# The last layer norm of an expert layer in three steps per unit, with GpSimd's instructions in a set order

## Chip, cores and metric

One core of one Trainium2 chip runs the whole program. The metric is the device time of one execution in microseconds (us). The engines are PE (TensorE), DVE (VectorE), ACT (ScalarE), POOL (GpSimd) and SP (SyncE, which issues plain DMAs). Each executes its own instructions in order, and the engines meet at semaphores.

## What is computed

Two transformer blocks on 2048 tokens of width 1024, all in float32. The first has chunked spatial gating, sliding-window attention and memory cross-attention, the second an mLSTM mixer, a memory cross-attention and a mixture of experts. The change touches only the experts' part and the layer norm behind it:

```
ff = grouped_moe(x, router_w, router_bias, w_gate, w_up, w_down)
x  = layer_norm(DEEPNORM_ALPHA * x + ff, ln_moe_g, ln_moe_b)
```

In `grouped_moe` every token first picks one of four groups of four experts, then two experts of that group. An expert is silu(x W_gate) * (x W_up), then W_down, with inner width 256. The sum is weighted by the two gates, added to ALPHA * x and normalized per token.

## The kernel before

The first part of the program (up to about 2230 us) works through blocks of 512 tokens and leaves three things in DRAM: `x3d` (input rows of the experts with their gates), `sumd` (ALPHA * x, onto which experts add), and tables of token numbers, 128 to a column. `moe()` then runs the experts.

**Units.** An expert has two or three blocks of 128 tokens (`BLOCKS`, 39 in all). Two blocks make a unit; a third block makes a short unit of its own that shares the expert's weights (`of`). There are 23 units, numbered 0 to 22. Units 5, 9, 13, 15, 17, 19 and 21 are short; unit 22 is expert 15, which has two blocks.

**One turn of the loop in `run`** handles unit i. PE does the first half of i's up projection (`up(0)`), then the second (`up(1)`), then the transposes of unit i+1, then the down projection of unit i-1. Around it stand, in program order: the down weights of unit i-1 (`weights_down(1)`) and of unit i; `mids[i]`; the activation; the gather of unit i+2 (`gather`, L1126, by indirect DMA from `x3d`); the scatter-add of unit i-1 onto `sumd` (L1201, one indirect DMA per block); `late[i]`; the up weights of unit i+2. Weights are split into two rounded parts: ACT casts (L173), DVE subtracts (L174). For `weights_down(1)` of experts 4 to 14 POOL subtracts.

**The last norm.** The tokens of experts 0 to 3 form list 0, those of 4 to 7 list 1, 8 to 11 list 2, 12 to 14 list 3, and all that picked expert 15 list 4. A list has `NFIN` static tiles of 128 rows; a list that is longer is finished in a loop behind, together with experts that have more tokens than their blocks hold. When a list's experts are all scattered, `group_done` makes its tiles ready. A tile costs one fetch from `sumd` (L1395, an indirect DMA by POOL), statistics (two L1410 and L1411 on DVE, or two ACT passes L1405 and L1406), the reciprocal root on POOL (`rstd_pow`, L192 and L194), two passes on DVE (L1417 and L1418, the second needs POOL's root) and a scatter to the output (L1419).

`last_norm`, called in `mids` or `late` about once per expert as the table `FETCH` says, finishes an older tile and fetches the next:

```python
            while got and got[0][0] <= t - lag:
                finish([got.pop(0)[1]])
            for _ in range(min(n, len(ready))):
                got.append((t, fetch(ready.pop(0), mem)))
```

**What sets the order.** ACT's and DVE's instructions of the experts' part stand as the program writes them (`manual_schedule` with `MANUAL`). Those of POOL, PE and SP are placed by the scheduler, within the dependencies. On `sumd` these are waits: a fetch waits until the scatter-adds issued before it have landed (`adds`), and a scatter-add waits until earlier scatter-adds and fetches have landed (`adds + reads`).

Of the kernel before, what the change touches and what calls it, by code (L numbers as in the profile page):

```python
# [17 lines left out]
OP = mybir.AluOpType  # L18
AX = mybir.AxisListType

D = 1024
S = 2048
# [5 lines left out]
LN_EPS = 1e-5  # L28
# [8 lines left out]
POOL_FIRST = 1  # L37
MANUAL = "Activation", "DVE"
BLOCKS = 2, 2, 2, 2, 3, 2, 2, 3, 2, 2, 3, 3, 3, 3, 3, 2
FETCH = {5: (1, 0), 6: (1, 0), 7: (1, 0), 8: (1, 0), 9: (1, 1), 10: (1, 0), 11: (1, 0), 12: (1, 0), 13: (1, 1), 14: (1, 1), 15: (1, 0)}  # L40


def f32(ap):
    return ap.bitcast(F32)
# [7 lines left out]
def model(ctx, tc, A, out, taps=None, nsb=NSB, upto=9):  # L52
# [116 lines left out]
    def split(hi, lo, src, lo_eng=None, hi_eng=None):  # L169
        if hi_eng is DVE:  # L170
            DVE.tensor_copy(hi, src)
        else:
            ACT.copy(hi, src)  # L173
        (lo_eng or DVE).tensor_sub(lo, src, f32(hi))  # L174

    def wload(src, w, lo_eng=None, into=None):
        raw = rawload(src, w)
# [9 lines left out]
        mm(o, lh, rl, False, False)  # L187
        mm(o, ll, rh, False, stop)

    def rstd_pow(src, eps, name, scale=1.0, n=1, bufs=3):  # L190
        v = sml([128, n], name + "v")
        POOL.tensor_scalar(v, src, scale, eps, op0=OP.mult, op1=OP.add)  # L192
        r = sml([128, n], name, bufs=bufs)
        POOL.tensor_tensor(r, v, mhalf[:, :n], op=OP.pow)  # L194
        return r

    pending = []
# [740 lines left out]
    NMAX = 28  # L938

    NL = 5  # L940
    NFIN = 4, 5, 5, 4, 2
    if upto >= 3:
        rw = cload("router_w", [128, 8, 16])
        rbias = const.tile([128, 16], F32, name="rbias")
# [139 lines left out]
    def moe():  # L1084
# [19 lines left out]
        def after(a, b):  # L1104
            tc.add_manual_dep(a.ins, b.ins.name, mybir.DependencyInfo(mybir.DependencyClass.Sync,
                                                                      mybir.DependencyReason.DATA), reason="same tokens")

        class Unit:


# [26 lines left out]
            def weights_down(self, f):  # L1137
                if self.of:
                    return
                raw = rawload(self.src_d(f), 1024)  # L1140
                h, l = DW((128, 1024)), DW((128, 1024))
                split(h, l, raw, POOL if self.late and f in LATE_POOL else self.lo)
                self.dw.append((h, l))

            def transposed(self):
# [43 lines left out]
            def down(self):  # L1189
                new = []  # L1190
                for r in range(self.n):
                    rs = slice(r * 128, (r + 1) * 128)
                    y = YT((128, D))
                    for hf in range(2):
                        hs = slice(hf * 512, (hf + 1) * 512)
                        a = acc()
                        for f in range(2):
                            h, l = self.dw[f]
                            mm3(a, self.th[:, f, rs], self.tl[:, f, rs], h[:, hs], l[:, hs], f == 0, f == 1)
                        ACT.activation(y[:, hs], a, AF.Copy, scale=self.gc[r])  # L1200
# [6 lines left out]
                    new.append(d)  # L1207
                adds[:] = new
                reads.clear()

        def run(units, early=None, mids={}, late={}, hooks={}):
            n = len(units)
            for j in range(min(2, n)):
                units[j].gather()
            units[0].weights_up(range(4))
            units[0].transposed()
            if early:
                early()
            if n > 1:
                units[1].weights_up(range(3))  # L1220
            for i, u in enumerate(units):
                v = units[i + 1] if i + 1 < n else None
                w = units[i + 2] if i + 2 < n else None
                u.up(0)
                if i:
                    units[i - 1].weights_down(1)
                u.weights_down(0)
                u.act(0)
                if i:
                    units[i - 1].turn()  # L1230
                if not v:
                    if i:
                        units[i - 1].down()
                    u.weights_down(1)
                if i in mids:
# [157 lines left out]
        def fetch(at, mem):  # L1393
            x = mem((128, D))
            d = POOL.indirect_dma_start(out=x, out_offset=None, in_=sumd[:, :], in_offset=at)  # L1395
            for o in adds:
                after(d, o)
            reads.append(d)
            return x, at

        def stats(x, on):
# [10 lines left out]
            return (mv[:, 0:1], OP.add if on is ACT else OP.subtract,  # L1412
                    rstd_pow(mv[:, 1:2], LN_EPS, "fr", scale=1.0 / D if on is ACT else 1.0))

        def finish(tiles, ons=(DVE,), static=True):
            for (x, at), (mean, op, r) in zip(tiles, [stats(x, on) for (x, at), on in zip(tiles, ons)]):
                DVE.scalar_tensor_tensor(x, x, mean, gains[:, 0], op0=op, op1=OP.mult)  # L1417
                DVE.scalar_tensor_tensor(x, x, r, gains[:, 1], op0=OP.mult, op1=OP.add)  # L1418
                d = POOL.indirect_dma_start(out=out[:, :], out_offset=at, in_=x, in_offset=None,  # L1419
                                            bounds_check=S - 1, oob_is_err=False)  # L1420
                for o in outs:
                    (apart if static else after)(d, o)
                outs.append(d)

        ready, got = [], []
# [5 lines left out]
        def last_norm(t, n, mem=FX, lag=2):  # L1431

            while got and got[0][0] <= t - lag:
                finish([got.pop(0)[1]])
            for _ in range(min(n, len(ready))):
                got.append((t, fetch(ready.pop(0), mem)))

        units, mids, late, hooks = [], {}, {}, {}
        for e in range(16):
            if e in FETCH and e < 15:  # L1440
                for j in range(2):
                    (late if j else mids)[len(units)] = lambda e=e, j=j: last_norm(2 * e + j, FETCH[e][j])
            units.append(static(e, 0, 2))
            if e in (4, 8, 12):
                hooks[len(units) - 1] = [lambda e=e: group_done((e - 1) // 4)]
            if BLOCKS[e] == 3:
                units.append(static(e, 2, 1, units[-1]))
        tables = [group_ranks, *(lambda j=j: place(range(4 * j, 4 * j + 4)) for j in range(4)), placed]
        for j, fn in enumerate(tables):
            mids[j] = fn  # L1450
        hooks.setdefault(5, []).append(overflow_table)
        hooks.setdefault(7, []).append(group_owners)

        def last():
            last_norm(30, 1)
            group_done(3)
            last_norm(0, NFIN[3], XG)

        mids[len(units) - 1] = last
        with tc.manual_schedule(engines={getattr(mybir.EngineType, e) for e in MANUAL}):  # L1460
            run(units, None, mids, late, hooks)
        group_done(4)
        last_norm(0, NFIN[4], MRAW)
        while got:
            finish([f for _, f in got[:2]], (DVE, ACT))
            del got[:2]
        assert not ready and not got


        nit = nc.values_load(ov["nit"][0:1, 0:1], min_val=0, max_val=NMAX)  # L1470
# [108 lines left out]
```

## Time and profile before

| what | value |
|---|---|
| median of three runs | 2713.98 us (2713.91, 2713.98, 2725.86) |
| the profiled execution | 2722.46 us, of which the span is 2720.7 us |
| busy in the span | PE 94%, DVE 59%, ACT 42%, POOL 22% |
| mean granted clock of TensorE | 0.972 of full speed |

The span runs from the first instruction to the last. Busy shares are means over the whole program; the part that the change touches is its last fifth. The profile names for each idle stretch what ended it. A TensorE clock of 1.00 is the level of 2.4 GHz, 0.50 that of 1.2 GHz; values between them are means over a stretch in which it was at both.

### The profile page before, as it was taken

The page shows a single profiled execution, that of the slowest core. Times are in us where ns is not written, and L with a number is a line of the kernel's source. Part 1 is how long each engine was busy: PE and PEld are TensorE (multiplying, and loading weights), DVE is VectorE, ACT ScalarE, POOL GpSimd, SP SyncE. Part 2 cuts the span into 40 slices and gives each one's busy share as a digit, 9 for nine tenths or more (in the row PEclk, how much of TensorE's full clock was granted, in tenths as well). Part 3 has the DMA queues.
Part 4 walks back from the last instruction along what each step waited for, and adds up shares of the span by engine and source line. Part 5 has one row for each costly group of instructions (what it writes and reads, how often), then busy time and mean ns, then how long its engine had stood idle before and what let it go on. Part 6 is the DMA issues. An engine that isn't in the chain of part 4 may idle for free. (4 is left out here: it accounts for less than half of the span.)

```text
span 2720.7 us, 36998 instructions
## 1 busy us (share of the span) xinstructions
PE 2549.0 (94%) x13954; PEld 2156.0 (79%) x13954; DVE 1608.8 (59%) x3228; ACT 1136.1 (42%) x2023; POOL 597.4 (22%) x635
## 2 busy tenths in 40 slices
PE   8899999999999999999999999999999969989882
PEld 8777788777878887778788878778888859978872
DVE  5536366766454666665456666563667457666554
ACT  5644353242444532434354333343532325444442
POOL 0102202211021031101201221021032133445445
PEclk9999999999999999999999999999999979999986
DMA  8861351444224325441242345312415357878755
GB/s 299 287 217 55 109 163 55 154 152 145 92 77 133 117 64 169 155 141 48 84 161 72 116 144 197 94 55 87 162 47 183 104 180 264 247 237 254 223 153 138
DMA packets 121557, 396.81 MB, mean 146 GB/s; under 512 B 15264, under 2 KB 15408, under 8 KB 121376
## 3 DMA queue, kind: packets, MB, share of 16 engines
q1 hardware_dynamic: 104144, 334.01, 36.6%
q0 software_dynamic: 17232, 60.42, 8.4%
q8 instruction: 110, 1.80, 0.3%
q14 instruction: 71, 0.58, 0.1%
HBM read 314.87 MB, written 81.60 MB: 146 GB/s over the span
## 5 line engine op out<-in xcount | busy, mean ns | idle before, releaser
L183 PE MATMUL bank<-rounded 128*128 128x512 f32 (+2 forms) x10628 | 2198.8, 364 | 73.4 <-ACT rounded L173 54.1
L183 PEld LDWEIGHTS bank<-rounded 128*128 128x128 f32 x10628 | 1773.3, 192 | 380.4 <-ACT rounded L173 61.5
L174 DVE TENSOR_TENSOR rounded<-work,rounded 128x1024 fp32r<-128x1024 f32 (+3 forms) x531 | 577.7, 1100 | 476.4 <-ACT rounded L173 430.4
L173 ACT CAST rounded<-work 128x1024 fp32r<-128x1024 f32 (+3 forms) x564 | 512.5, 926 | 691.2 <-PE bank L183 251.8
L173 ACT CAST rounded<-bank 128x512 fp32r<-128x512 f32 (+1 forms) x220 | 112.0, 555 | 219.1 <-PE bank L240 98.1
L183 PE MATMUL bank<-work 128*128 128x128 f32 (+5 forms) x944 | 163.6, 301 | 6.9 <-DVE work L525 2.2
L183 PEld LDWEIGHTS bank<-work 128*128 128x128 f32 (+1 forms) x944 | 130.7, 190 | 37.0 <-issue 5.1
L174 DVE TENSOR_TENSOR rounded<-bank,rounded 128x512 fp32r<-128x512 f32 (+1 forms) x220 | 133.0, 639 | 42.5 <-ACT rounded L173 40.6
L240 PE MATMUL bank<-ident,work 128*128 128x128 f32 x712 | 98.2, 283 | 28.4 <-ACT work L345 8.6
L240 PEld LDWEIGHTS bank<-ident,work 128*128 128x128 f32 x712 | 82.2, 145 | 46.3 <-ACT work L345 13.4
L192 POOL TENSOR_SCALAR lnrv<-lnmv 128x1 f32<-128x1 f32 x32 | 40.6, 1269 | 283.3 <-DVE lnmv L672 283.1
L375 POOL TENSOR_SCALAR work<-work 128x512 f32<-128x512 f32 x32 | 25.4, 793 | 345.9 <-ACT work L374 345.9
L665 DVE SCALAR_TENSOR_TENSOR work<-work,bank 128x512 f32<-128x512 f32 x64 | 43.8, 685 | 73.3 <-PE bank L183 73.1
L1201 POOL DMA_INDIRECT sumd<-work,tabi x39 | 72.1, 1849 | 35.1 <-ACT work L1200 15.7
L174 POOL TENSOR_TENSOR rounded<-work,rounded 128x1024 fp32r<-128x1024 f32 (+1 forms) x33 | 65.9, 1997 | 38.1 <-ACT rounded L173 35.4
L754 DVE SCALAR_TENSOR_TENSOR work<-work,c_convT 128x512 f32<-128x512 f32 x96 | 71.9, 749 | 2.5 <-ACT work L752 0.7
L1126 POOL DMA_INDIRECT work<-x3d,tabi x39 | 47.9, 1228 | 113.9 <-issue 42.1
L859 POOL TENSOR_TENSOR work<-work 128x512 f32<-128x512 f32 (+6 forms) x40 | 46.2, 1154 | 112.3 <-ACT work L851 110.4
L192 POOL TENSOR_SCALAR rrmsv<-ssq 128x1 f32<-128x1 f32 x34 | 11.2, 329 | 261.4 <-DVE ssq L570 172.7
L795 POOL TENSOR_TENSOR work<-work,ar 128x520 f32<-128x520 f32 x16 | 17.0, 1062 | 232.8 <-DVE work L757 177.3
L906 POOL TENSOR_SCALAR work<-work,xrv 128x256 f32<-128x256 f32 x64 | 30.1, 484 | 152.3 <-DVE xrv L904 152.3
L1200 ACT ACTIVATE work<-bank,gr 128x512 f32<-128x512 f32 x78 | 51.1, 702 | 29.4 <-PE bank L183 13.0
(320 smaller groups left out, 2148.1 us busy)
## 6 DMA issues: line engine op xcount, KB each, us to landing
work<-in_w_gu SPq DMA_DIRECT2D x64, 512.0 KB
work<-in_x SPq DMA_DIRECT2D x32, 512.0 KB
work<-in_w_out SPq DMA_DIRECT2D x32, 512.0 KB
work<-wmp SPq DMA_DIRECT2D x32, 512.0 KB
work<-wxa SPq DMA_DIRECT2D x32, 512.0 KB
work<-wvw SPq DMA_DIRECT2D x32, 512.0 KB
work<-in_w_dn SPq DMA_DIRECT2D x32, 512.0 KB
sumd<-work SPq DMA_DIRECT2D x19, 512.0 KB
```

The source lines that it names most:

```text
L173: ACT.copy(hi, src)
L174: (lo_eng or DVE).tensor_sub(lo, src, f32(hi))
L183: PE.matmul(o, l, r, start=start, stop=stop)
L192: POOL.tensor_scalar(v, src, scale, eps, op0=OP.mult, op1=OP.add)
L240: PE.transpose(p[:, k * 128:(k + 1) * 128], src[:, (4 * hf + k) * 128:(4 * hf + k + 1) * 128], ident)
L665: DVE.scalar_tensor_tensor(oh_, xr, ALPHA, a, op0=OP.mult, op1=OP.add)
L754: DVE.scalar_tensor_tensor(s, z[:, k:k + T], conv[:, k, c:c + 1], s, op0=OP.mult, op1=OP.add)
L859: POOL.tensor_tensor(nx[:, lo:], cur[:, lo:], cur[:, lo - d_:15 + T - d_], op=OP.add)
L906: POOL.tensor_scalar(P[:, h, :], P[:, h, :], rv[:, h:h + 1], 0.0, op0=OP.mult, op1=OP.add)
L1126: POOL.indirect_dma_start(out=xg, out_offset=None, in_=x3d[:, :], in_offset=at)
L1200: ACT.activation(y[:, hs], a, AF.Copy, scale=self.gc[r])
L1201: d = POOL.indirect_dma_start(out=sumd[:, :], out_offset=self.at[r], in_=y, in_offset=None, compute_op=OP.add)
```

## The change

The tables `FETCH` and the function `last_norm` go. In their place, in each unit from 5 on: `measure` at `mids` (statistics and POOL's root of the tile fetched one unit earlier), one fetch at the new place `turn` (behind unit i+1's transposes, ahead of the gather), and `norms` at `late` (the two DVE passes and the scatter to the output). So up to one tile is fetched per unit, where it was about one per expert.

`queued` chains POOL's instructions of the loop: each gather, `weights_down(1)` subtraction, scatter-add, fetch, root and output scatter is placed behind the one before it in program order, without a wait of its own.

`NFIN` goes from 4, 5, 5, 4, 2 to 3, 5, 5, 3, 2. With the inputs of `setup_inputs` the reference's routing puts 380, 546, 550, 382 and 190 tokens on the five lists, so lists 0 and 3 just fit in three tiles.

```diff
-FETCH = {5: (1, 0), 6: (1, 0), ..., 9: (1, 1), ..., 13: (1, 1), 14: (1, 1), 15: (1, 0)}
-    def rstd_pow(src, eps, name, scale=1.0, n=1, bufs=3):
+    def rstd_pow(src, eps, name, scale=1.0, n=1, bufs=3, then=None):
...
-        POOL.tensor_tensor(r, v, mhalf[:, :n], op=OP.pow)
+        d = POOL.tensor_tensor(r, v, mhalf[:, :n], op=OP.pow)
+        if then:
+            then(d)
-    NFIN = 4, 5, 5, 4, 2
+    NFIN = 3, 5, 5, 3, 2
+        line = [[], []]
+        def queued(*ds_):
+            if line[0]:
+                for d in ds_:
+                    for o in line[1]:
+                        tc.add_manual_dep(d.ins, o.ins.name, mybir.DependencyInfo(
+                            mybir.DependencyClass.NoSync, mybir.DependencyReason.DATA), reason="order")
+            line[1] = ds_
+            return ds_[0]
...
-                    POOL.indirect_dma_start(out=xg, out_offset=None, in_=x3d[:, :], in_offset=at)
+                    queued(POOL.indirect_dma_start(out=xg, out_offset=None, in_=x3d[:, :], in_offset=at))
...
                     v.weights_up([3])
+                    if i in turn:
+                        turn[i]()
                     if w:
                         w.gather()
...
+        def scaled(x, at, mean, op, r, static=True):
+            DVE.scalar_tensor_tensor(x, x, mean, gains[:, 0], op0=op, op1=OP.mult)
+            DVE.scalar_tensor_tensor(x, x, r, gains[:, 1], op0=OP.mult, op1=OP.add)
+            d = POOL.indirect_dma_start(out=out[:, :], out_offset=at, in_=x, in_offset=None,
+                                        bounds_check=S - 1, oob_is_err=False)
...
+        def measure():
+            while got:
+                x, at = got.pop(0)
+                measured.append((x, at, *stats(x, DVE)))
+        def fetches(n, mem=FX):
             for _ in range(min(n, len(ready))):
-                got.append((t, fetch(ready.pop(0), mem)))
+                got.append(fetch(ready.pop(0), mem))
+        def norms():
+            while measured:
+                scaled(*measured.pop(0))
+        for j in range(5, len(units) - 1):
+            mids[j], turn[j], late[j] = measure, lambda: fetches(1), norms
...
         def last():
-            last_norm(30, 1)
+            measure()
+            norms()
             group_done(3)
-            last_norm(0, NFIN[3], XG)
+            fetches(NFIN[3], XG)
```

How the instructions stand. `bank_66` and the like are PSUM banks, `fmv` a tile's mean and variance, `fr` its reciprocal root, `gr` a gate, `rounded` a split half of weights or activations. Line numbers of the changed kernel are its own: L173 is its subtraction, L1139 its gather, L1217 its scatter-add, L1414 its fetch, L191 and L193 its root, L1435 and L1436 its DVE passes, L1437 its output scatter.

DVE in unit 12 (the activation of both halves of an expert with the norm between), before:

```order
L1175 SCALAR_TENSOR_TENSOR work<-work,bank_66 128x256
L1176 TENSOR_TENSOR work<-work,bank_66 128x256
L174 TENSOR_TENSOR rounded<-work,rounded 128x256
L1410 BN_STATS fst_17211<-work 128x6 x2
L1411 BN_AGGR fmv_17209<-fst_17211 128x2
L1417 SCALAR_TENSOR_TENSOR work<-work,fmv_17209 128x1024
L1418 SCALAR_TENSOR_TENSOR work<-work,fr_17221 128x1024
L1175 SCALAR_TENSOR_TENSOR work<-work,bank_67 128x256
L1176 TENSOR_TENSOR work<-work,bank_67 128x256
L174 TENSOR_TENSOR rounded<-work,rounded 128x256
L174 TENSOR_TENSOR rounded<-bank_68,rounded 128x512
L174 TENSOR_TENSOR rounded<-bank_69,rounded 128x512
```

and with the change:

```order
L1429 BN_STATS fst_17045<-work 128x6 x2
L1430 BN_AGGR fmv_17041<-fst_17045 128x2
L1191 SCALAR_TENSOR_TENSOR work<-work,bank_67 128x256
L1192 TENSOR_TENSOR work<-work,bank_67 128x256
L173 TENSOR_TENSOR rounded<-work,rounded 128x256
L173 TENSOR_TENSOR rounded<-bank_68,rounded 128x512
L173 TENSOR_TENSOR rounded<-bank_69,rounded 128x512
L1319 COPY gr_15868<-work 128x1
L1435 SCALAR_TENSOR_TENSOR work<-work,fmv_17041 128x1024
L1436 SCALAR_TENSOR_TENSOR work<-work,fr_17053 128x1024
L173 TENSOR_TENSOR rounded<-work,rounded 128x1024 x3
```

The two passes of the norm have moved from ahead of the second activation to behind the splits of the next unit's transposes.

POOL in the same unit, before:

```order
L174 TENSOR_TENSOR rounded<-work,rounded 128x1024
L1126 DMA work<-x3d,tabi 128x1040
L1395 DMA work<-sumd,tab 128x1024 x2
L192 TENSOR_SCALAR frv_17217<-fmv_17209 128x1
L194 TENSOR_TENSOR fr_17221<-frv_17217,mhalf 128x1
L1419 DMA out_dram<-work,tab 2048x1024
L1126 DMA work<-x3d,tabi 128x1040
L1201 DMA sumd<-work,tabi 2432x1024
```

and with the change:

```order
L173 TENSOR_TENSOR rounded<-work,rounded 128x1024
L191 TENSOR_SCALAR frv_17049<-fmv_17041 128x1
L193 TENSOR_TENSOR fr_17053<-frv_17049,mhalf 128x1
L1414 DMA work<-sumd,tab 128x1024
L1139 DMA work<-x3d,tabi 128x1040 x2
L1217 DMA sumd<-work,tabi 2432x1024 x2
L1437 DMA out_dram<-work,tab 2048x1024
```

The root of a tile now stands ahead of the fetch of the next; the gather stands behind that fetch.

POOL in units 14 and 15, a pair of a full and a short unit, before:

```order
L1126 DMA work<-x3d,tabi 128x1040
L1201 DMA sumd<-work,tabi 2432x1024
L174 TENSOR_TENSOR rounded<-work,rounded 128x1024
L1126 DMA work<-x3d,tabi 128x1040
L1201 DMA sumd<-work,tabi 2432x1024
L1126 DMA work<-x3d,tabi 128x1040
L1201 DMA sumd<-work,tabi 2432x1024
L1395 DMA work<-sumd,tab 128x1024
```

and with the change:

```order
L1414 DMA work<-sumd,tab 128x1024
L1139 DMA work<-x3d,tabi 128x1040 x2
L1217 DMA sumd<-work,tabi 2432x1024
L1437 DMA out_dram<-work,tab 2048x1024
L173 TENSOR_TENSOR rounded<-work,rounded 128x1024
L191 TENSOR_SCALAR frv_17049<-fmv_17041 128x1
L193 TENSOR_TENSOR fr_17053<-frv_17049,mhalf 128x1
L1414 DMA work<-sumd,tab 128x1024
L1139 DMA work<-x3d,tabi 128x1040
L1217 DMA sumd<-work,tabi 2432x1024 x2
```

Where there was one fetch for the pair there are two, and each scatter-add of the pair has a fetch ahead of it.

## Rows read from the trace of the kernel before

**Rows 1.** Windows: stretch and length, busy us (instructions) per engine, PEclk, DMA share, GB/s.

```profile
2300.00:2350.00 50.00, 50.00 (x360) 47.13 (x360) 29.60 (x62) 26.60 (x43) 19.65 (x14) 1.00 0.85 249
...
2450.00:2500.00 50.00, 45.64 (x311) 42.74 (x310) 33.72 (x45) 21.19 (x37) 28.28 (x24) 0.93 0.75 223
...
2650.00:2700.00 50.00, 22.54 (x135) 19.21 (x133) 23.72 (x31) 15.11 (x27) 27.43 (x30) 0.76 0.64 158
```

**Rows 2.** Waits from 2240 us on: total us, times, longest.

```profile
POOL work L1395 <- DMA sumd<-work,tabi: 59.5, 10, 10.0
DVE work L1418 <- POOL fr L194: 49.3, 15, 6.9
...
PE bank L183 <- ACT rounded L173: 37.1, 10, 7.7
...
PE bank L183 <- POOL rounded L174: 5.9, 2, 3.9
```

**Rows 3.** Timeline of POOL in unit 12: start, us, instruction, idle before and its end.

```profile
2482.68 0.96 POOL L1395 DMA_INDIRECT work<-sumd,tab  x1 [4.80 <-DMA sumd<-work,tabi]
2483.94 0.94 POOL L1395 DMA_INDIRECT work<-sumd,tab  x1 [0.30 <-issue]
...
2485.22 0.57 POOL L194 TENSOR_TENSOR fr<-frv,mhalf 128x1 f32<-128x1 f32 x1
```

**Rows 4.** Timeline of DVE in unit 12.

```profile
2485.83 1.28 DVE L1418 SCALAR_TENSOR_TENSOR work<-work,fr 128x1024 f32<-128x1024 f32 x1 [6.08 <-POOL fr L194]
```

**Rows 5.** Timeline of PE, units 5 to 22; L1186 is the transposes of a short unit.

```profile
2352.26 0.38 PE L1186 MATMUL bank<-ident,work 128*128 128x128 f32 x2
...
2488.88 8.81 PE L183 MATMUL bank<-rounded 128*128 128x256 f32 x48 [3.99 <-ACT rounded L173]
...
2512.77 0.38 PE L1186 MATMUL bank<-ident,work 128*128 128x128 f32 x2
...
2548.75 6.00 PE L183 MATMUL bank<-rounded 128*128 128x256 f32 x48
2554.59 1.04 PE L240 MATMUL bank<-ident,work 128*128 128x128 f32 x8
2555.38 2.99 PE L183 MATMUL bank<-rounded 128*128 128x512 f32 x12
...
2567.20 1.91 PE L240 MATMUL bank<-ident,work 128*128 128x128 f32 x16
2568.87 11.46 PE L183 MATMUL bank<-rounded 128*128 128x512 f32 x72
...
2642.37 13.43 PE L183 MATMUL bank<-rounded 128*128 128x512 f32 x68 [3.91 <-POOL rounded L174]
2655.64 0.38 PE L1186 MATMUL bank<-ident,work 128*128 128x128 f32 x2
...
2675.20 5.11 PE L183 MATMUL bank<-rounded 128*128 128x512 f32 x12 [7.71 <-ACT rounded L173]
```

**Rows 6.** By line, in this order: scatter-add L1201, fetch L1395, gather L1126.

```profile
DMA to landing us min/median/max: 6.4/8.9/12.0
...
DMA to landing us min/median/max: 4.2/5.2/6.2
...
DMA to landing us min/median/max: 5.9/8.3/10.9
```

**Rows 7.** Timeline of POOL around a fetch that a scatter-add waited for.

```profile
2606.60 0.99 POOL L1395 DMA_INDIRECT work<-sumd,tab  x1 [4.86 <-DMA sumd<-work,tabi]
...
2613.32 1.59 POOL L1201 DMA_INDIRECT sumd<-work,tabi  x1 [4.47 <-DMA work<-sumd,tab]
2615.22 1.57 POOL L1201 DMA_INDIRECT sumd<-work,tabi  x1 [0.30 <-issue]
```

**Rows 8.** Timeline of POOL behind the last unit.

```profile
2668.13 1.00 POOL L1395 DMA_INDIRECT work<-sumd,tab  x1 [4.70 <-DMA sumd<-work,tabi]
...
2695.00 1.00 POOL L1395 DMA_INDIRECT work<-sumd,tab  x1 [3.81 <-issue]
```

More of the change, by code (lines that the diff above doesn't have):

```diff
@@ L39 @@
 BLOCKS = 2, 2, 2, 2, 3, 2, 2, 3, 2, 2, 3, 3, 3, 3, 3, 2
-FETCH = {5: (1, 0), 6: (1, 0), 7: (1, 0), 8: (1, 0), 9: (1, 1), 10: (1, 0), 11: (1, 0), 12: (1, 0), 13: (1, 1), 14: (1, 1), 15: (1, 0)}
 def f32(ap):
@@ L173, in split @@
             ACT.copy(hi, src)
-        (lo_eng or DVE).tensor_sub(lo, src, f32(hi))
+        return (lo_eng or DVE).tensor_sub(lo, src, f32(hi))
     def wload(src, w, lo_eng=None, into=None):
@@ L1141, in weights_down @@
                 h, l = DW((128, 1024)), DW((128, 1024))
-                split(h, l, raw, POOL if self.late and f in LATE_POOL else self.lo)
+                on = POOL if self.late and f in LATE_POOL else self.lo
+                d = split(h, l, raw, on)
+                if on is POOL:
+                    queued(d)
                 self.dw.append((h, l))
@@ L1207, in down, with run @@
                     new.append(d)
+                queued(*new)
                 adds[:] = new
                 reads.clear()
-        def run(units, early=None, mids={}, late={}, hooks={}):
+        def run(units, early=None, mids={}, turn={}, late={}, hooks={}):
             n = len(units)
@@ L1397, in fetch @@
                 after(d, o)
-            reads.append(d)
+            reads.append(queued(d))
             return x, at
@@ L1411, in stats @@
                 DVE.bn_aggr(mv, st)
-            return (mv[:, 0:1], OP.add if on is ACT else OP.subtract,
-                    rstd_pow(mv[:, 1:2], LN_EPS, "fr", scale=1.0 / D if on is ACT else 1.0))
-        def finish(tiles, ons=(DVE,), static=True):
[L1416 to L1425, printed above, removed]
+            r = rstd_pow(mv[:, 1:2], LN_EPS, "fr", scale=1.0 / D if on is ACT else 1.0, then=queued)
+            return mv[:, 0:1], OP.add if on is ACT else OP.subtract, r
+        def scaled(x, at, mean, op, r, static=True):
[3 more added lines that the diff above has]
+                                        bounds_check=S - 1, oob_is_err=False)
+            for o in outs:
+                (apart if static else after)(d, o)
+            outs.append(d)
+            if static:
+                queued(d)
+        def finish(tiles, ons=(DVE,), static=True):
+            for (x, at), s in zip(tiles, [stats(x, on) for (x, at), on in zip(tiles, ons)]):
+                scaled(x, at, *s, static=static)
+        ready, got, measured = [], [], []
         def group_done(g):
@@ L1429, in group_done @@
                 ready.append(bass.IndirectOffsetOnAxis(ap=tabgi[:, g * 16 + c:g * 16 + c + 1], axis=0))
-        def last_norm(t, n, mem=FX, lag=2):
-            while got and got[0][0] <= t - lag:
-                finish([got.pop(0)[1]])
-            for _ in range(min(n, len(ready))):
-                got.append((t, fetch(ready.pop(0), mem)))
-        units, mids, late, hooks = [], {}, {}, {}
+        def measure():
[3 more added lines that the diff above has]
+        def fetches(n, mem=FX):
+            for _ in range(min(n, len(ready))):
+                got.append(fetch(ready.pop(0), mem))
+        def norms():
+            while measured:
+                scaled(*measured.pop(0))
+        units, mids, turn, late, hooks = [], {}, {}, {}, {}
         for e in range(16):
-            if e in FETCH and e < 15:
-                for j in range(2):
-                    (late if j else mids)[len(units)] = lambda e=e, j=j: last_norm(2 * e + j, FETCH[e][j])
             units.append(static(e, 0, 2))
@@ L1450, in moe @@
             mids[j] = fn
+        assert len(tables) == 6
         hooks.setdefault(5, []).append(overflow_table)
@@ L1454, in last @@
         def last():
-            last_norm(30, 1)
+            measure()
+            norms()
             group_done(3)
-            last_norm(0, NFIN[3], XG)
+            fetches(NFIN[3], XG)
         mids[len(units) - 1] = last
         with tc.manual_schedule(engines={getattr(mybir.EngineType, e) for e in MANUAL}):
-            run(units, None, mids, late, hooks)
-        group_done(4)
-        last_norm(0, NFIN[4], MRAW)
+            line[0] = True
+            run(units, None, mids, turn, late, hooks)
+            line[0] = False
+            assert not ready
+            group_done(4)
+            fetches(NFIN[4], MRAW)
         while got:
-            finish([f for _, f in got[:2]], (DVE, ACT))
+            finish(got[:2], (DVE, ACT))
             del got[:2]
-        assert not ready and not got
         nit = nc.values_load(ov["nit"][0:1, 0:1], min_val=0, max_val=NMAX)
```

## Prediction

> **What bounds the kernel now.** I read the windows first. In the experts' part PE can run without a pause: between 2300 and 2350 us it is busy for all of 50.00 us at a granted clock of 1.00. Later, once the last norm runs beside the experts, it is busy for 45.6 of 50 us at a mean of 0.93, and near the end for 22.5 us at 0.76 [rows 1]. So PE is the bound and is made to wait. The waits say by whom: from 2240 us on PE sat idle 37.1 us for ACT's casts and 5.9 us for POOL's weight subtraction; DVE waited 49.3 us in 15 places for the root that POOL computes, and POOL 59.5 us with a fetch for scatter-adds to land [rows 2].
>
> The timelines of unit 12 join these into one chain. POOL's queue holds the next tiles' fetches, which wait for a scatter-add until 2482.68, ahead of the root of a tile whose statistics are long there; the root comes at 2485.22 [rows 3]. DVE, in order, has waited 6.08 us for it when L1418 starts at 2485.83 [rows 4]. Behind L1418 stand the second activation and the splits of the next unit's transposes, and PE starts that unit at 2488.88, 3.05 us later, after a gap of 3.99 us [rows 5]. The same pattern stands at six other units, with waits of up to 6.9 us [rows 2]. A gap costs twice: the 48 matmuls behind this one take 8.81 us, where 48 without a gap take 6.00 [rows 5], because the clock has fallen to the level of 1.2 GHz for a while.
>
> **What PE's own work needs.** From rows 5: 48 matmuls of one up half-pair 6.00 us (a full unit has 96, a short one 48), transposes 1.91 for two blocks and 1.04 for one, a down projection 2.99 for one block and 11.46 - 6.00 = 5.46 for two, and 0.38 for a short unit's extra transposes.
> - Units 6 to 13 (six full, two short): 84.0 + 13.5 + 38.7 + 0.8 = 137.0. It took 2512.77 - 2352.26 = 160.5, so 23.5 are lost.
> - Units 14 to 21 (four pairs of a full and a short one): 72.0 + 11.8 + 33.8 + 1.5 = 119.1, or 29.8 per pair. It took 142.9; lost 23.8.
> - From the transposes of unit 21 to PE's end at 2680.3: 14.8 of work in 24.7, lost 9.9, with 7.71 in one gap [rows 5].
> - Behind it 40.4 us to the end of the span.
>
> **The change, part by part.**
> 1. *Root ahead of the fetch, passes behind the transposes' splits.* The root no longer waits for the fetch, and L1417 and L1418 (1.28 us each) with any wait of theirs stand behind what PE needs next. What DVE holds up now is the split of weights for a unit further on and the next activation, with a down projection of 3 to 5.5 us and an up half to cover it. If the cover is gone, each late pass costs what it did. In and just before units 6 to 13 only six tiles are fetched (units 5 to 7 and 11 to 13), mostly beside full units. I leave 4.5 of the 23.5 for small gaps: **-19**.
> 2. *One fetch per unit instead of one per expert.* This puts a round trip on POOL that is not in the old order: scatter-add, landing, fetch, landing, next scatter-add. A fetch with the wait behind it takes 2613.32 - 2606.60 = 6.7 us, the second scatter-add of a full unit follows 1.9 later [rows 7], and the landing before the next fetch is 8.9 in the middle [rows 6]. A pair needs 6.7 + 1.9 + 8.9 + 6.7 + 8.9 + 0.6 of issue = 33.7 us, against PE's 29.8. The excess falls on the short units, where the loop needs 17.8 and PE 13.4. Late next is the gather, now queued behind the fetch: in a full unit the fetch starts at about 9.2, two gathers 1.3 apart follow, landing takes 8.3 [rows 6], so data is there at 20.1 and wanted at 16.4 + 6.0 = 22.4. POOL's subtraction of down weights behind the scatter-add is late by about as much, beside it. So some 2 us of lag are free, and units 15, 19 and 21 wait for 3 to 5 us each; the list runs dry in units 8 to 10 and 16, where the loop catches up. I take 12 us, by the median rows. Both ends: with the shortest landings the loop is 4.2 + 1.9 + 6.4 + 4.2 + 6.4 + 0.6 = 23.7 per pair and costs nothing; with the longest, 6.7 + 1.9 + 12.0 + 6.7 + 12.0 + 0.6 = 39.9, some 10 per pair and 36 in all.
>    The Trainium skill, "DMA: Bandwidth & Descriptors", section "Anatomy of one DMA", gives a GpSimd DMA about 2.0 us and its bytes at 436 KB per us, an estimate of 3.2 us for one of these 512 KB; by it the loop would be far inside PE's time and this term zero. The traced 5.2 and 8.9 [rows 6] disagree, and I go by them.
> 3. *Clock after those waits.* Three gaps of 3 to 5 us; the one shown cost 2.8 us besides itself [rows 5], a shorter one less: 4, and 2 for small gaps. Units 14 to 21 then lose 12 + 4 + 2 = 18 instead of 23.8: **-6**. The two waits for POOL's subtraction (5.9 in all, one the 3.91 before the matmuls at 2642.37) are in the old 23.8 and in the new 12.
> 4. *Last unit and tail.* The norm in unit 22 is still finished ahead of the activation, and its root now stands behind unit 21's scatter-add, which waits for unit 20's to land. I give back half of the 9.9. Of what follows PE's end, the chain is scatter-add, fetch of list 4, norm, output, as before; the last fetch at 2695.00 leaves 25.7 us to the end [rows 8]; one tile fewer is left in it for DVE's two passes (2 x 1.28 [rows 4]), 3 us less. But the three fetches of list 3 start only when unit 21's scatter-add has landed, as at 2668.13 [rows 8]. Together **-4**, between -10 and +3.
> 5. *Two tiles fewer*: two fetches, roots and output scatters and 2 x 2.6 us of passes on DVE with their statistics, in the tail and in units that wait for other things. Counted in 4; elsewhere nothing, hidden behind PE. The chaining itself adds no wait and no instruction.
>
> Sum: -19 - 6 - 4 = **-29**. Against the profiled execution that is 2722.5 - 29 = 2693.5. The median of the runs shown is 8.5 below that execution; I apply the same difference to it: 2714 - 29 = **2685 us**.
>
> **Rivals.**
> - *The round trip never ends last* (landings as short as the shortest rows, since each list's traffic is spread over more units). Then units 14 to 21 keep only small gaps, -22, and the tail does better by up to 6: -19 - 22 - 8 = -49, 2665 us. For it: in the old trace the scatter-adds that a fetch waits for often overlap another, and the short ones land in 6.4. Against it: the median is 8.9 at a DMA load that rises. This is the case that the Trainium skill's figure named in part 2 would give.
> - *The round trip ends last nearly everywhere* (landings near 12 us). Waits of 36 us with 8 of clock lost put units 14 to 21 at +20 against before; with -19 and the tail at 0 the time is 2714 + 1 = 2715 us. For it: DMA is already busy for 0.75 to 0.85 of the stretch [rows 1]. Against it: the two runs of fetches are five units each, so the lag has little time to grow.
> - *A list overflows*, the slower case. Lists 0 and 3 hold 384 rows for 380 and 382 tokens. If the kernel's own routing puts three more tokens on list 3 than the reference does, the loop behind runs once, for an empty expert block and the list's rest, all in series: gather 8.3, transposes, up and down about 11, scatter-add 8.9, two fetches 5.2 each, two norms of about 5 each, output landing about 6 as the longest fetch, some 55 us estimated from [rows 4 to 6]: 2740 us. Up to two more, nothing happens. Against it: the old kernel, with lists that can't tell, says nothing of 380 or 382, but routing moves only where two scores tie almost exactly.
> - *The change doesn't do what it says*: the order of the instructions shows that it does, on DVE and POOL.
>
> **How the numbers follow.** About 0.5% (13.6 us, so 2700.4 and 2727.5) is what a measurement of this kernel can tell from no change. Chances: the forecast with 6 to 20 us of waits, 2675 to 2702, 0.55; no round trip bound, 2658 to 2675, 0.20; round trip everywhere, 2702 to 2725, 0.17; overflow 0.05; something that these rows don't show and that makes it slower 0.03. Of the forecast 0.52 lie below 2700.4. Faster 0.72, same 0.20, slower 0.08. The range reaches from 2664, where half of the first rival is left out, to 2712, where half of the second is.
>
> **What would show it.** Right: DVE's wait for POOL's root falls from 49.3 to under 20 us, with little of it before an up projection; units 6 to 13 take 140 to 143 us; PE's gaps stand in units 15, 19 and 21, ended by POOL's gather or subtraction, 12 us in all; a fetch follows each scatter-add of units 11 to 15 and 17 to 21 by its landing. Wrong in 1: gaps remain at the start of full units with ACT's cast as their end. Wrong in 2: no gaps in short units, or gaps above 8 us. Wrong in 4: the last fetch comes more than 12 us earlier or any later against PE's end. An overflow would show gathers beyond 39.

## The result and the profile after

The changed kernel takes 2677.71 us (median of four runs, 2670.2 to 2679.76) where the kernel before takes 2718.27 us, the median with a fourth run. The measured ratio is 0.9839, with a 95% interval of 0.9813 to 0.9865; like the other ratios here it goes by all the runs and is not the quotient of the two medians (0.9851). A later comparison gave 0.9844 [0.982, 0.9867], 2676.57 us. The forecast was 2685 us, 29 less than before; it is some 41 less. The profiled execution after took 2679.76 us, its span 2678.0 us at a mean granted clock of 0.979. Against the profiled execution of before the span is 42.7 us shorter.

Windows of the kernel after, columns as in [rows 1]:

```profile
2450.00:2500.00 50.00, 50.00 (x362) 47.30 (x361) 32.95 (x52) 25.16 (x43) 27.61 (x22) 1.00 0.86 235
2500.00:2550.00 50.00, 44.34 (x293) 40.98 (x292) 32.55 (x51) 24.86 (x41) 27.04 (x22) 0.90 0.87 262
```

The stretch in which PE was busy for 45.64 us at a clock of 0.93 [rows 1] is now without a pause at a clock of 1.00, and DMA is busier in it (0.86 for 0.75). The stretch behind it still has pauses. Waits of the kernel after from 2240 us on, as in [rows 2]:

```profile
POOL work L1414 <- DMA sumd<-work,tabi: 25.9, 8, 5.1
...
POOL sumd L1217 <- DMA work<-sumd,tab: 21.1, 5, 5.8
PE bank L241 <- DMA work<-x3d,tabi: 10.5, 6, 4.0
...
DVE work L1436 <- POOL fr L193: 5.1, 6, 2.0
PE bank L182 <- ACT rounded L172: 5.1, 3, 2.5
...
PE bank L182 <- POOL rounded L173: 1.4, 1, 1.4
```

DVE's wait for the root fell from 49.3 us to 5.1, and PE's for ACT's casts from 37.1 to 5.1. A new wait has come: PE for the gather (L241 transposes the gathered rows), 10.5 us; and scatter-adds wait 21.1 us for fetches, where it was one wait of 4.47 [rows 7]. PE's timeline after shows where. All its gaps of over 0.3 us behind 2366 us are here. L1202 transposes the activation of a short unit, early in the next unit's turn; its rows for units 5, 9, 13, 15, 17 and 21 serve as marks:

```profile
2351.49 0.38 PE L1202 MATMUL bank<-ident,work 128*128 128x128 f32 x2
...
2422.48 0.38 PE L1202 MATMUL bank<-ident,work 128*128 128x128 f32 x2
...
2488.23 0.38 PE L1202 MATMUL bank<-ident,work 128*128 128x128 f32 x2
...
2507.67 1.97 PE L241 MATMUL bank<-ident,work 128*128 128x128 f32 x8 [3.95 <-DMA work<-x3d,tabi]
...
2511.35 1.97 PE L241 MATMUL bank<-ident,work 128*128 128x128 f32 x8 [1.71 <-DMA work<-x3d,tabi]
2512.97 12.87 PE L182 MATMUL bank<-rounded 128*128 128x512 f32 x72
2525.68 0.38 PE L1202 MATMUL bank<-ident,work 128*128 128x128 f32 x2
...
2553.98 0.38 PE L1202 MATMUL bank<-ident,work 128*128 128x128 f32 x2
...
2573.81 1.84 PE L241 MATMUL bank<-ident,work 128*128 128x128 f32 x8 [3.11 <-DMA work<-x3d,tabi]
...
2603.77 1.09 PE L241 MATMUL bank<-ident,work 128*128 128x128 f32 x8 [0.67 <-DMA work<-x3d,tabi]
2605.25 1.09 PE L241 MATMUL bank<-ident,work 128*128 128x128 f32 x8 [0.39 <-DMA work<-x3d,tabi]
...
2608.64 10.59 PE L182 MATMUL bank<-rounded 128*128 128x512 f32 x68 [1.37 <-POOL rounded L173]
2619.07 0.38 PE L1202 MATMUL bank<-ident,work 128*128 128x128 f32 x2
...
2633.47 3.01 PE L182 MATMUL bank<-rounded 128*128 128x512 f32 x12 [2.52 <-ACT rounded L172]
```

From unit 5's mark to unit 13's, 136.7 us, there are only three small gaps in the first 15 us (3.0 in all). From there to unit 21's, 130.8 us, the gaps are in units 15, 19 and 21 and add up to 11.2 us. POOL's timeline at the first of them:

```profile
2498.53 1.58 POOL L1414 DMA_INDIRECT work<-sumd,tab  x1 [5.14 <-DMA sumd<-work,tabi]
2500.41 1.01 POOL L1139 DMA_INDIRECT work<-x3d,tabi  x1 [0.30 <-issue]
2501.72 1.94 POOL L1139 DMA_INDIRECT work<-x3d,tabi  x1 [0.30 <-issue]
```

The fetch waits 5.14 us for a scatter-add to land, the gathers stand behind it, and PE gets their rows at 2507.67 and 2511.35.

For the comparisons the span is cut at the same places in each kernel: at the marks of units 5, 13 and 21, and at PE's end (the last end on PE's timeline). Each row of these tables is one execution. The stretch up to unit 5, where the kernels hardly differ, varies by 7 us among them, so spans are to be compared with that in mind, and the ratios go by more runs. In us:

| kernel | up to unit 5 | units 6–13 | units 14–21 | last unit | behind PE | span |
|---|---|---|---|---|---|---|
| before | 2352.3 | 160.5 | 142.9 | 24.7 | 40.4 | 2720.7 |
| after | 2351.5 | 136.7 | 130.8 | 17.4 | 41.5 | 2678.0 |

### The profile page after: what moved, and what is told of

It is laid out like the page before. It is cut to its first block, busy times and chain, and to the rows that moved or that the text cites. A ratio compares the mean times of both kernels' runs of the same rounds, so it can differ in the third digit from the quotient of the medians.

```text
span 2678.0 us, 36955 instructions
## 1 busy us (share of the span) xinstructions
PE 2533.3 (95%) x13954; PEld 2146.2 (80%) x13954; DVE 1604.4 (60%) x3224; ACT 1133.4 (42%) x2015; POOL 590.2 (22%) x627
## 5 line engine op out<-in xcount | busy, mean ns | idle before, releaser
L173 DVE TENSOR_TENSOR rounded<-work,rounded 128x1024 fp32r<-128x1024 f32 (+3 forms) x531 | 579.0, 1102 | 464.3 <-ACT rounded L172 414.8
L173 DVE TENSOR_TENSOR rounded<-bank,rounded 128x512 fp32r<-128x512 f32 (+1 forms) x220 | 133.6, 640 | 48.4 <-ACT rounded L172 46.9
L241 PE MATMUL bank<-ident,work 128*128 128x128 f32 x712 | 100.4, 287 | 37.0 <-DMA work<-x3d,tabi 16.0
L241 PEld LDWEIGHTS bank<-ident,work 128*128 128x128 f32 x712 | 83.6, 147 | 55.6 <-DMA work<-x3d,tabi 18.4
L191 POOL TENSOR_SCALAR lnrv<-lnmv 128x1 f32<-128x1 f32 x32 | 40.6, 1268 | 286.7 <-DVE lnmv L673 286.6
L1217 POOL DMA_INDIRECT sumd<-work,tabi x39 | 66.5, 1705 | 109.9 <-ACT work L1216 72.3
L173 POOL TENSOR_TENSOR rounded<-work,rounded 128x1024 fp32r<-128x1024 f32 (+1 forms) x33 | 65.2, 1977 | 58.4 <-ACT rounded L172 55.7
L191 POOL TENSOR_SCALAR rrmsv<-ssq 128x1 f32<-128x1 f32 x34 | 10.0, 294 | 262.8 <-DVE ssq L571 172.7
L1216 ACT ACTIVATE work<-bank,gr 128x512 f32<-128x512 f32 x78 | 52.5, 699 | 29.2 <-PE bank L182 19.9
L564 ACT COPY work<-bank 128x512 f32<-128x512 f32 x32 | 18.8, 587 | 84.6 <-PE bank L182 84.6
```

Source lines behind the costliest of these rows:

```text
L173: return (lo_eng or DVE).tensor_sub(lo, src, f32(hi))
L241: PE.transpose(p[:, k * 128:(k + 1) * 128], src[:, (4 * hf + k) * 128:(4 * hf + k + 1) * 128], ident)
```

## Experiments: the three parts, alone and together

The change has three parts: the split of the norm, the chain on POOL, and fewer list tiles. The split always comes with the new places of the fetches, one per unit; the split with the old rate of fetches was not tried. The theory: the split removes the gaps at the starts of units, the chain only carries it, and the two tiles are worth little. The rival: the chain does the work, by taking the placement of POOL's instructions from the scheduler. Six variants beside the two kernels make all eight combinations.

**Fewer tiles alone**, on the kernel before:

```diff
-    NFIN = 4, 5, 5, 4, 2
+    NFIN = 3, 5, 5, 3, 2
```

> The kernel before with the shorter lists alone (3, 5, 5, 3, 2). Theory (order: DVE waited for POOL's root, which stood behind a waiting fetch): two tiles fewer are worth 3 to 8 us, DVE's wait for the root stays above 40 us, PE's gaps at the start of full units stay. Rival (less work: the two tiles carry the gain): 20 us or more faster than before.

Measured: 2704.35 us, 0.9947 [0.9931, 0.9962], some 14 us, which is more than the first theory allowed and less than the other wanted. Its waits:

```profile
DVE work L1418 <- POOL fr L194: 37.5, 16, 5.0
...
PE bank L183 <- ACT rounded L173: 21.7, 10, 7.5
```

Two tiles fewer took 15.4 us of PE's 37.1 [rows 2] away. List 3's tiles are fetched in the last unit, so only one tile less is finished beside the experts: POOL issues 12 fetches ahead of the last unit instead of 13. The fetch at 2438.32 before has no counterpart here, and the gap of 7.24 us on PE behind it has become 0.99. In the old order a tile that is finished beside the experts can make a gap, and this one did. Two other gaps, of 3.99 and 4.91 us, have become 0.63 and 0.65 although their tiles are still finished there; why was not tried.

**The old list sizes in the changed kernel** (the same edit backwards):

> The changed kernel with the old lists (4, 5, 5, 4, 2). Theory (order): 3 to 8 us slower than the changed kernel, DVE's wait for the root stays under 10 us. Rival (less work): back to within 10 us of the kernel before.

Measured: 2682.57 us, 0.9869 [0.9841, 0.9897]. That is 5 us more than after by the medians, 8 by the ratios, with intervals that overlap, and DVE waits 7.8 us for the root, as the first theory said. Where the gaps are gone anyway, two tiles are worth little.

**Chain alone**, on the kernel before: `queued` at all its places, `line[0] = True` around the units, no split.

> The kernel before with the chain on POOL alone: root, output scatter, fetch in program order, passes still ahead of the second activation. Theory B (the root's place): DVE's wait for the root falls under 20 us and most of the gain is there, 20 us or more faster than before. Theory A (the passes' place): DVE's wait falls too, but the passes still delay each activation; less than 15 us faster than before.

Measured: 2715.52 us, 0.9990 [0.9977, 1.0003]: no gain that can be told. The waits show what became of the gaps (L1436 is its second DVE pass, L183 the matmul):

```profile
DVE work L1436 <- POOL fr L194: 28.5, 15, 8.1
PE bank L183 <- POOL rounded L174: 21.0, 5, 7.7
...
PE bank L183 <- ACT rounded L173: 7.3, 4, 3.3
```

PE waits 29.8 us less for ACT and 15.1 more for POOL's subtraction. The root is mostly in time: on DVE's timeline 11 of the 15 waits for it last 0.75 us or less. Late is the subtraction, which the chain holds in program order behind a fetch that waits. POOL, and PE behind it:

```profile
2597.92 0.98 POOL L1413 DMA_INDIRECT work<-sumd,tab  x1 [8.65 <-DMA sumd<-work,tabi]
2598.93 2.35 POOL L174 TENSOR_TENSOR rounded<-work,rounded 128x1024 fp32r<-128x1024 f32 x1
```

```profile
2601.33 10.89 PE L183 MATMUL bank<-rounded 128*128 128x512 f32 x63 [7.66 <-POOL rounded L174]
```

Of the five gaps that the subtraction ends, three of the four long ones have such a fetch just ahead of it; the fourth has an output scatter there. What PE gains all the same is half lost behind its end: PE ends 13.8 us earlier than before, and the stretch behind it is 7.0 longer (table below). The rival falls: the chain without the split gains next to nothing.

**No chain in the changed kernel**:

```diff
-            line[0] = True
             run(units, None, mids, turn, late, hooks)
```

> The changed kernel without the chain on POOL; the scheduler then puts most fetches ahead of the root again. Theory A (what counts is that the passes stand behind what PE needs): DVE's wait for the root comes back to 30 us or more, but PE's gaps do not; 0 to 10 us slower than the changed kernel. Theory B (what counts is the root's place on POOL): the gaps come back, 20 us or more slower than the changed kernel.

Measured: 2689.09 us, 0.9900 [0.9873, 0.9927]: 11 us lost by the medians, some 16 by the ratios, between the theories. DVE's wait for the root is back at 41.1 us and units 6 to 13 hardly notice (139.6 us), as theory A says; but against it PE has gaps again, of 6.37, 3.92 and 9.96 us in units 15, 19 and 21, ended by POOL's subtraction, and 9.44 in the last unit.

**Split alone**: the same edit, with the old list sizes.

> The split of the norm (statistics and root, then the fetch, then the two passes behind the next unit's transposes) alone: no chain on POOL, and lists of 4, 5, 5, 4, 2 tiles as before. Measured so far against before: fewer lists alone -14 us, chain alone -4, split with chain -36, split with fewer lists -30, all three -41. If the parts add up, split alone is -16 to -32 by the one or the other pair: 2688 to 2704 us, DVE's wait for the root about 41 us as without the chain. If the split is worth nothing without one of the other two, -5 or less, 2714 us or more, and DVE's wait for the root stays near 49 us.

Measured: 2697.34 us, 0.9933 [0.9908, 0.9958], on the same chip as a repeat of the changed kernel at 0.9844. The time lies in the range given for parts that add up, and the wait near the 41 us given; by stages the parts do not add up, as the table below shows. Its waits and, below, the gaps of over 3 us on its PE:

```profile
DVE work L1436 <- POOL fr L193: 38.2, 11, 5.6
PE bank L182 <- POOL rounded L173: 23.7, 4, 10.0
PE bank L182 <- ACT rounded L172: 10.2, 2, 9.4
```

```profile
2512.72 12.96 PE L182 MATMUL bank<-rounded 128*128 128x512 f32 x68 [7.19 <-POOL rounded L173]
...
2577.40 13.07 PE L182 MATMUL bank<-rounded 128*128 128x512 f32 x68 [5.18 <-POOL rounded L173]
...
2618.51 13.00 PE L182 MATMUL bank<-rounded 128*128 128x512 f32 x68 [10.00 <-POOL rounded L173]
...
2652.56 5.44 PE L182 MATMUL bank<-rounded 128*128 128x512 f32 x12 [9.35 <-ACT rounded L172]
```

DVE still waits 38.2 us for the root, because the scheduler, left alone, again places fetches ahead of roots. Only one of these 11 waits is in units 6 to 13, and it is hidden: on DVE's timeline it lasts 5.25 us, beside a PE that does not pause.

```profile
2486.56 1.29 DVE L1436 SCALAR_TENSOR_TENSOR work<-work,fr 128x1024 f32<-128x1024 f32 x1 [5.25 <-POOL fr L193]
```

In units 14 to 21 there are six, 23.9 us in all, and yet no gap of PE there is ended by DVE or by ACT: all three are ended by POOL's subtraction. So behind the splits DVE's waits did no harm here, and units 6 to 13 take 136.1 us without any chain. In the last unit the passes still stand ahead of the activation: there DVE waits 4.86 us for the root, and PE's gap of 9.35 follows. What else is missing is in units 15, 19 and 21, where a waiting fetch is ahead of the subtraction of down weights on POOL; its timeline in front of the 10.00 us gap:

```profile
2614.78 1.30 POOL L1414 DMA_INDIRECT work<-sumd,tab  x1 [4.02 <-DMA sumd<-work,tabi]
2616.07 2.38 POOL L173 TENSOR_TENSOR rounded<-work,rounded 128x1024 fp32r<-128x1024 f32 x1
```

In unit 21 the chain places the subtraction and the root ahead of that fetch. In units 15 and 19 a fetch is ahead of the subtraction in either order, with other issues between them. There the fetch goes out earlier with the chain (split and chain, old lists): 9.1 us behind the mark of unit 13 and 8.4 behind that of 17, instead of 14.6 and 12.6. In the free order a gather stands between the two scatter-adds that this fetch waits for (2489.89, gather 2491.81, 2493.10); that this alone makes the difference was not shown.

**Chain and fewer tiles**, on the kernel before:

> Chain and fewer lists on the kernel before, without the split. If they add up: -14 - 4 = -18 us, 2701 us. If the chain's loss (root behind fetch, and the longer time behind PE's end) grows or shrinks with the number of tiles: -8 or less (2711 us or more) or -25 (2694 us). In all cases DVE still waits over 20 us for the root, since the program order puts it behind the fetch; if that wait falls under 10, the split is not what removes it.

Measured: 2706.74 us, 0.9965 [0.9951, 0.9978], some 10 us: less than the sum of both, and the root is waited for as expected (32.2 us).

| kernel | up to unit 5 | units 6–13 | units 14–21 | last unit | behind PE | span | ratio |
|---|---|---|---|---|---|---|---|
| tiles | 2346.3 | 151.6 | 134.2 | 25.5 | 38.5 | 2696.1 | 0.9947 |
| chain | 2352.6 | 160.5 | 136.1 | 17.3 | 47.4 | 2713.9 | 0.9990 |
| chain, tiles | 2350.1 | 154.4 | 137.8 | 18.9 | 43.0 | 2704.2 | 0.9965 |
| split | 2351.3 | 136.1 | 144.0 | 26.7 | 35.7 | 2693.7 | 0.9933 |
| split, tiles | 2346.8 | 139.6 | 141.7 | 26.8 | 32.2 | 2687.1 | 0.9900 |
| split, chain | 2353.6 | 138.5 | 125.6 | 18.8 | 44.2 | 2680.6 | 0.9869 |

The split takes all it can from units 6 to 13 (24.4 us) and nothing from units 14 to 21. The chain, once the split is there, takes 18.4 from units 14 to 21 and 7.9 from the last unit, and gives 8.5 back behind PE. So the chain pays only with the split, and the split pays nearly twice as much with the chain: 0.67% and 0.10% apart, 1.31% together.

## Experiments: what holds the changed kernel

**The passes early again**: roots stay ahead of the fetch, the two DVE passes go back ahead of the second activation.

```diff
-            mids[j], turn[j], late[j] = measure, lambda: fetches(1), norms
+            mids[j], turn[j] = lambda: (measure(), norms()), lambda: fetches(1)
```

> The changed kernel with the two passes and the output scatter back at the place of the statistics, ahead of the second activation; chain, fetch per unit and lists as changed. Theory A (the passes' place counts): 13 tiles delay an activation by about 4 us each, of which PE sees 1 to 2; 13 to 26 us slower than the changed kernel. Theory B (only the root's place counts): under 8 us slower.

Measured: 2683.38 us, 0.9869 [0.9843, 0.9895], 6 to 8 us more than after, with intervals that overlap; that is on theory B's side. Units 6 to 13 take 143.5 us, 17.0 less than before. With the root in time the passes' old place costs little; split alone showed the reverse, that with the root left behind the fetches the new place costs units 6 to 13 nothing. Either of the two removes most of what step 1 of the prediction is about.

**The gather ahead of the fetch**, with **POOL's subtraction on DVE**, and both:

```diff
-                    if i in turn:
-                        turn[i]()
                     if w:
                         w.gather()
+                    if i in turn:
+                        turn[i]()
```

```diff
-LATE_POOL = (1,)
+LATE_POOL = ()
```

> The changed kernel with the gather ahead of the fetch in each unit. Theory (round trip: the gather behind a waiting fetch is what PE waits for in units 15, 19 and 21): PE's waits for x3d in those units vanish, 3 to 9 us faster than the changed kernel, less if POOL's subtraction of down weights is then what PE waits for there. Rival (the gather itself is slow to land under load): the waits stay.

> The changed kernel with the subtraction of all down weights on DVE. Theory (round trip): POOL's queue is 2.5 us shorter per expert but the fetch still waits for landings, so PE's waits for the gather stay; within 4 us of the changed kernel. Rival (POOL's own work, not the landings, makes the gather late): 5 us or more faster.

> Both of the last two edits. Theory (round trip): nothing that PE needs stands behind a fetch any more, PE's waits in units 13 to 21 fall from about 11 us to under 3, 6 to 12 us faster than the changed kernel. Rival (DVE has no room for the subtractions): new waits of PE for DVE's splits, no gain.

Measured: gather first 2682.18 us, 0.9864 [0.9846, 0.9882]; subtraction on DVE 2674.97 us, 0.9837 [0.9816, 0.9858]; both 2679.45 us, 0.9868 [0.9840, 0.9896]. The subtraction on DVE stayed within the 4 us expected. The gains expected of the gather first (3 to 9 us) and of both (6 to 12) did not come. With the gather first, PE waits 0.8 us for rows instead of 10.5; in unit 15 POOL's queue runs into the same round trip one instruction later. The scatter-add here may go only when the fetch ahead of it has landed. The profile names no releaser for it, but its own rows are there when ACT's L1216 ends at 2504.96, and DVE's statistics, which wait for that fetch, start at 2515.26, just ahead of it. POOL, and that row of DVE:

```profile
2506.89 1.46 POOL L1414 DMA_INDIRECT work<-sumd,tab  x1 [1.06 <-DMA sumd<-work,tabi]
2516.00 1.61 POOL L1217 DMA_INDIRECT sumd<-work,tabi  x1 [7.65 <-issue]
2517.91 1.02 POOL L1437 DMA_INDIRECT out_dram<-work,tab  x1 [0.30 <-DVE rounded L173]
2518.94 2.38 POOL L173 TENSOR_TENSOR rounded<-work,rounded 128x1024 fp32r<-128x1024 f32 x1
```

```profile
2515.26 1.29 DVE L1429 BATCH_NORM_STATS2 fst<-work 128x6 f32<-128x512 f32 x2 [4.93 <-DMA work<-sumd,tab]
```

and PE, in its own timeline, waits for the subtraction:

```profile
2521.37 13.36 PE L182 MATMUL bank<-rounded 128*128 128x512 f32 x68 [8.27 <-POOL rounded L173]
```

With both edits the short units' waits are small (units 14 to 21 take 123.5 us), but units 6 to 13 take 138.9, with a wait of 2.60 us for gathered rows at 2367.26, and the last unit 21.4, with this gap on PE:

```profile
2629.87 4.61 PE L182 MATMUL bank<-rounded 128*128 128x512 f32 x12 [4.97 <-ACT rounded L172]
```

Why those two waits come was not tried. The same edit of the subtraction was then run beside the changed kernel on one chip:

> The changed kernel itself, run beside the variant with the subtraction on DVE on one chip. 2672 to 2680 us.

> The changed kernel with the late subtraction of down weights on DVE in place of POOL. If POOL's chain still costs something in the changed kernel (subtraction behind scatter-adds, fetch behind subtraction), it is 2 to 6 us faster than the changed kernel on the same chip; if the round trip of scatter-add and fetch is all that is left, the two agree within 2 us.

Measured: 0.9844 [0.9820, 0.9867] for the changed kernel, 0.9848 [0.9824, 0.9872] with the subtraction on DVE. They agree, and PE's wait for the gather is still there (12.8 us; 11.6 in the changed kernel). No version tried is clearly faster than the changed kernel.

## Why the prediction was right, and where it was off

Mechanism and sign held, and the time fell in the range; the sum was -29 and the traces of the two profiled executions show -42.7 (the medians of the runs 40.6). What PE loses to waits and clock was sized within 1 us in units 6 to 13 and in units 14 to 21. The term that was mis-sized is PE's own work, which the prediction subtracts from each stretch to get what is lost there. By its steps:

- **Step 1**, -19 forecast, -23.8 measured. The place was right. The work of PE can be read where it has no gap, at a clock of 1.00: from the mark of unit 9 to that of unit 13 three full units and a short one take 65.75 us, so units 6 to 13 need 131.5. The prediction reckoned 137.0, since it added up durations of rows that overlap: in [rows 5] the row behind 48 matmuls of 6.00 us starts 5.84 after them, the row behind transposes of 1.91 us 1.67 after them. Units 6 to 13 took 136.7, so 5.2 were lost, 3.0 of them in the three gaps; 4.5 had been left for that. Of the signs set for this step, DVE's wait for the root under 20 us was met (5.1) but proves less than it seemed: split alone misses it at 38.2 us and has the whole gain of these units. The other, 140 to 143 us for units 6 to 13, was missed by the overcounted work.
- **Step 2**, 12 us of waits forecast, 11.2 measured, in the units named and by the releasers named (gather five times, subtraction once). The round trip is what ends these waits: moving the gather ahead of the fetch only moved the wait to POOL's subtraction. Its length was forecast as 33.7 us per pair of units; from a fetch to the one a pair later POOL took 34.6 and 32.9:

```profile
2562.55 1.04 POOL L1414 DMA_INDIRECT work<-sumd,tab  x1 [3.41 <-DMA sumd<-work,tabi]
...
2578.84 1.75 POOL L1414 DMA_INDIRECT work<-sumd,tab  x1 [4.10 <-DMA sumd<-work,tabi]
...
2597.16 1.06 POOL L1414 DMA_INDIRECT work<-sumd,tab  x1 [4.40 <-DMA sumd<-work,tabi]
...
2611.71 1.85 POOL L1414 DMA_INDIRECT work<-sumd,tab  x1 [0.40 <-issue]
```

  The landings spread more than before (scatter-add 6.1 to 13.7 us, gather 4.3 to 15.0), so a sum by median rows was lucky in part. The Trainium skill, "DMA: Bandwidth & Descriptors", section "Anatomy of one DMA", gives about 2.0 us and the bytes at 436 KB per us, an estimate of 3.2 us for these 512 KB. The trace disagrees: the shortest fetch took 4.3 us, the median one 5.3, the median scatter-add 8.3.
- **Step 3**, clock and small gaps, 6 us forecast, about 6 paid. The one pair without a gap, units 16 and 17, takes 28.3 us between its marks (2525.68, 2553.98), so four pairs need 113.2; the prediction had 119.1, by the same overlaps. Units 14 to 21 took 130.8, so 17.6 were lost: 11.2 in gaps and 6.4 in what follows them, slow stretches above all, against 18 forecast. Two groups of eight transposes took 1.97 us and one 1.84, where 1.04 is full speed (the granted clock is 0.50 from 2507.67 to 2513.00), and 72 matmuls 12.87, where 11.46 is. So steps 2 and 3 together gave -12.0 instead of -6 because the work was counted 5.9 too high. With the 5.5 of step 1 that is 11.4 of the 13.7 us between forecast and trace: with PE's work read from stretches without a gap, the same terms sum to about -40.
- **Step 4**, -4 forecast, -6.2 measured: the last unit 7.3 less, the stretch behind PE 1.1 more. The sign set for it failed: the fetch of list 4, which the prediction calls the last, stands 17.7 us behind PE's end (2654.13 against 2636.5), where it was 14.7 before. POOL's timeline says why:

```profile
2633.84 1.03 POOL L1414 DMA_INDIRECT work<-sumd,tab  x1 [0.30 <-DMA sumd<-work,tabi]
...
2644.26 1.63 POOL L1217 DMA_INDIRECT sumd<-work,tabi  x1 [2.38 <-DMA work<-sumd,tab]
...
2654.13 1.05 POOL L1414 DMA_INDIRECT work<-sumd,tab  x1 [1.96 <-issue]
```

  Unit 22's scatter-add goes out 7.8 us after PE's end, since it waits for list 3's fetches, and those came only after unit 21's scatter-add. PE finishes earlier than this loop can, so a part of what the last unit gains is lost behind it. Fetching list 3 behind unit 22's scatter-add was not tried.
- **Step 5**, two tiles at nothing outside the tail, and a chain that adds nothing. The tiles are worth 14 us in the old kernel and 5 to 8 in the new one, so nothing was wrong for the old one and low for the new one. The prediction gave the chain no term of its own, since it priced the changed order as a whole; that hides what the chain does. The split alone has gaps of 7.19, 5.18, 10.00 and 9.35 us; with the chain (old lists) no gap of PE behind unit 13 is over 2.4 us.
- The rest, -0.8, lies ahead of unit 5.

Of the **rivals**, the round trip that never ends last (2665 us) did not come: 11.2 us of it were paid. The time alone, between that rival and the forecast, could not have told them apart; the gaps on PE's timeline do. The round trip that ends last nearly everywhere did not come, since it shows in three of the four pairs of units with at most 5.7 us each. No list overflowed: the trace has 39 gathers, one per block, and no loop behind.

## What to carry to other kernels

A wait on an in-order engine costs what stands behind it: moving it behind the work that the bound engine needs next did here what removing it would (23.9 us of DVE's waits in units 14 to 21 ended no gap of PE). Where the scheduler placed one queue freely, waiting DMA issues stood ahead of short operations that others needed, so the edit of program order paid in full only with that queue's order fixed too; fixing the old order paid next to nothing. Parts of a change need not add up (split and chain 0.67% and 0.10% alone, 1.31% together; tiles and chain 0.53% and 0.10% alone, 0.35% together), so try them in combination before one is dropped. And take an engine's own work from a stretch without gaps: durations of neighbouring rows can overlap, and here adding them up hid 11.4 us of loss.

## What the runs showed of the hardware

Behind long gaps the length of the gap hardly mattered for what it cost besides itself: the 68 matmuls that take 10.59 us behind a gap of 1.37 us took 12.96, 13.07 and 13.00 behind gaps of 7.19, 5.18 and 10.00, and 13.43 behind one of 3.91 [rows 5]. Landing times spread more than the rows of before had shown, and their median moved the other way: a gather took 4.3 to 15.0 us with a median of 6.3, where it was 5.9 to 10.9 with a median of 8.3 [rows 6].
